# An encoder trunk in one core: the first weight sum of the second layer moves from VectorE to an accumulating transfer

## The chip, the cores and the metric

The kernel runs on one core of one Trainium2 chip. The metric is device time in microseconds (us) for one execution of the whole program, given as the median of several executions. Beside it one execution was recorded by the hardware profiler; its page and trace are what the numbers below come from. The engines are named as the profile names them: PE is TensorE (matmuls), PEld its weight loads, DVE is VectorE, ACT is ScalarE, POOL is GpSimd, SP is SyncE, which here only issues transfers.

## The reference

A two-layer encoder on 512 tokens of width 1024, all in float32. Each layer normalizes the tokens, multiplies them by one wide input matrix, runs a token mixer and an attention into 256 memory tokens, gates the result and adds an output projection:

```python
for i in range(DEPTH):
    h = rmsnorm(x, norm_g[i])
    mem_h = rmsnorm(mem, mem_norm_g[i])
    if i % 2 == 0:
        proj = jnp.einsum('bsd,de->bse', h, w_in_a[j])
        ...
        o_mix = mixer_dilated(qkv, qn_a[j], kn_a[j], ang_a)
    else:
        proj = jnp.einsum('bsd,de->bse', h, w_in_b[j])
        ...
        o_mix = mixer_axial_gqa(proj[..., :c1], proj[..., c1:c2], proj[..., c2:c3],
                                qn_b[j], kn_b[j], ang_b)
    o_mem = memory_attention(q_mem, mem_h, w_mem_kv[i], mem_qn_g[i], mem_kn_g[i])
    y = jnp.concatenate([o_mix, o_mem], axis=-1) * jax.nn.silu(gate)
    x = x + jnp.einsum('bse,ed->bsd', y, w_out[i])
```

The change touches only how the weight matrices of the second layer (`w_in_b` and `w_out[1]`) are prepared for the matmuls.

## The kernel before

**Products.** Float32 accuracy is reached by splitting each operand into a rounded part and a rest: `mm3` (lines 146 to 149) makes three matmuls, rounded by rounded (L147), and the two mixed ones (L148, L149). Most projections are computed in `s_chunk` (line 326) as a two-by-two block product with seven block products in place of eight, in the manner of Strassen and Winograd. That needs sums of the four quarters of a weight matrix. With the quarters called 21, 11, 12 and 22, the sums are T1 = 12 + 11, T2 = 22 + T1, T3 = 12 + 22 and T4 = 21 + T2. The seven products use the operands in the order 21, 11, T1, T2, 22, T3, T4, one after the other; each product of a 512-column chunk is one *group* of 24 matmuls, and PE runs through the groups without a break if nothing is late.

**Chunks.** `PLAN` (line 36) lists the weight chunks in order. The chunks are counted from 0. In the second layer, chunks 20 to 26 (kind W1b) are 512 columns of the input matrix each, in the order memory query, keys and values, two chunks of queries and three of gate; chunk 27 (kind W2b, 1024 columns, two tiles to a quarter) is the first two thirds of the output projection. Chunks 17 and below belong to the first layer; 18, 19, 28 and 29 take no sums.

**Weight pieces.** The class `Weights` keeps a clock `g` that counts groups. `advance` (line 288) is called once per group and puts into the program, in this order: the rest of an earlier piece (`lo`), at most one sum (`sum`), one rounding (`hi`), and the loads (`dma`). A piece of 128x1024 goes through these steps:

- a load from DRAM by SP into a tile `wl` (L217);
- for a sum, the addition into that tile: T1 on DVE (L231); T2 as an accumulating transfer from the T1 tile, issued by POOL (L236); T3 as an accumulating transfer straight from DRAM, issued by POOL (L241); T4 as an accumulating transfer of T2 into the tile of 21 (L246);
- the rounding by ACT into `wh` (L262), two or more groups before the product;
- the rest, `wl - wh`, by DVE into `wo` (L272).

`ripe` (line 219) sets how many groups must lie between a step and the next in the program: `LEAD`, which is 2, after a transfer, and 1 after the DVE sum T1. This is only the order in which instructions are written; at run time each instruction waits by semaphore for what it reads. Every engine works through its own instructions in the written order.

**What else the engines do.** The results of a group leave PSUM through ACT copies (L334) and DVE additions (L344). Head norms take squares on ACT (L495), the inverse root on POOL (L385, L386) and a multiplication on DVE (L500). Rotary terms (L1231 to L1236), softmax (L1280, L1284, L1289, L1290, L1299 to L1308), gates (L698 to L716) and the sums for the output projection (L736 to L762) run between the groups, given out slot by slot by the class `Driver`. POOL's line of work in the second layer is the inverse roots, the rotary table (L1177) and the issuing of T2, T3 and T4, all in one order.

Of the kernel before, what the change touches and what calls it, by code (L numbers as in the profile page):

```python
# [13 lines left out]
ALU = mybir.AluOpType  # L14
# [19 lines left out]
A_ORDER = "01234567mab"  # L34

PLAN = ["W2"] + ["T2"] * 2 + ["W1", "W2s"] + ["W2" if c.isdigit() else "W1" for c in A_ORDER[1:]] + ["W2"] + ["O1"] * 2 + ["T2b"] * 2 + ["W1b"] * 7 + ["W2b"] + ["O1"] * 2
KEEP = {"T2": 6, "T2b": 4, "O1": 4, "W1": 9, "W2": 10, "W2s": 9, "W1b": 7, "W2b": 9}


# [69 lines left out]
def trunk_kernel(ctx: ExitStack, tc: tile.TileContext, x, mem, wall, norm_g, mem_norm_g, gcol,  # L109
                 qn_a, kn_a, qn_b, kn_b, ident_d, mask_d, tab_a, tab_b, out):  # L110
    nc = tc.nc
    V, A, G, T = nc.vector, nc.scalar, nc.gpsimd, nc.tensor
# [26 lines left out]
    def split(hi, lo, src, act=True):  # L139
        if act:  # L140
            A.copy(hi, src)  # L141
        else:
            V.tensor_copy(hi, src)
        V.tensor_tensor(lo, src, hi.bitcast(F32), ALU.subtract)  # L144
# [16 lines left out]
    class Weights:  # L161
        def __init__(self):
            self.items, self.last, self.need, self.allocs, self.sums = [], [], [], [], []
            self.users = {}
            d = g = 0
            for c, kind in enumerate(PLAN):
                base = len(self.items)
                if kind in GROUPS:
                    units, nb = GROUPS[kind]
                    for u in range(units):  # L170
                        for x in (2 * u, 2 * u + 1):
                            self.items.append((c, "P", x))
                            self.last.append(g + (u + 1) * nb - 1)
                            self.allocs.append(((c, "P", x), d, kind))
                            self.users[c, "P", x] = 1
                            d += 1
                        self.need += [base + 2 * u + 2] * nb
                    g += units * nb
                else:
                    n = 1 if kind in ("W1", "W1b") else 2  # L180
                    at = {k: d + i * n for i, k in enumerate(("21", "11", "12", "22"))}
                    d += 4 * n
                    self.allocs += [((c, k, x), at[q] + x, kind) for k, q in LOADS for x in range(n)]
                    for k in ORDER:
                        for x in range(n):
                            self.items.append((c, k, x))
                            self.last.append(g)
                            self.need.append(len(self.items))
                            if k[0] == "T":
                                self.sums.append(((c, k, x), at["22"] + x))  # L190
                            if k != "T4":
                                self.users[c, k, x] = 1 if k in ("22", "T3") else 2
                            g += 1
            assert d == wall.shape[0], (d, wall.shape)
            self.g = -1
            self.live = 0
            self.tile, self.load_at, self.at, self.lo_at = {}, {}, {}, {}
            self.n_hi = self.n_lo = self.taken = 0
            self.op, self.hi_at = [], []
# [8 lines left out]
        def dma(self, most=9):  # L208
            while self.allocs and self.live < KEEP[self.allocs[0][2]] and most:
                most -= 1  # L210
                key, d, _ = self.allocs.pop(0)
                self.live += 1
                self.tile[key] = m4(name="wl")
                self.load_at[key] = self.g
                if key[1][0] != "T":
                    self.at[key] = self.g
                nc.sync.dma_start(self.tile[key], wall[d])  # L217
# [4 lines left out]
        def sum(self, force=False, want=None):  # L222

            for n, (key, d) in enumerate(self.sums[:8]):
                if want and key != want:
                    continue
                c, k, x = key
                if k == "T1":
                    if not (self.ripe(self.load_at, key, force) and self.ripe(self.at, (c, "11", x), force)):
                        continue  # L230
                    V.tensor_tensor(self.tile[key], self.tile[key], self.tile[c, "11", x], ALU.add)  # L231
                    self.use((c, "11", x))
                elif k == "T2":
                    if not (self.ripe(self.load_at, key, force) and self.ripe(self.at, (c, "T1", x), force, 1)):
                        continue
                    G.dma_start(self.tile[key], self.tile[c, "T1", x], accum_op=ALU.add)  # L236
                    self.use((c, "T1", x))
                elif k == "T3":
                    if not self.ripe(self.load_at, key, force):
                        continue  # L240
                    G.dma_start(self.tile[key], wall[d], accum_op=ALU.add)  # L241
                else:
                    if not (self.ripe(self.lo_at, (c, "21", x), force, 1) and self.ripe(self.at, (c, "T2", x), force)):
                        continue
                    self.tile[key] = self.tile[c, "21", x]
                    G.dma_start(self.tile[key], self.tile[c, "T2", x], accum_op=ALU.add)  # L246
                    self.use((c, "T2", x))
                self.at[key] = self.g
                self.sums.pop(n)
                return True  # L250
            return False

        def hi(self, force=False):
            i = self.n_hi
            if i >= len(self.items) or not self.ripe(self.at, self.items[i], force, 1 if self.items[i][1] == "T1" else None):
                return False
            if i >= RING and self.last[i - RING] > self.g:
                return False
            self.n_hi += 1
            wh = pool.tile([128, 1024], F32R, tag="wh", name="wh", bufs=RING)  # L260
            wo = pool.tile([128, 1024], F32R, tag="wo", name="wo", bufs=RING)
            A.copy(wh, self.tile[self.items[i]])  # L262
            self.hi_at.append(self.g)
            self.op.append((wh, wo))
            return True
# [1201 lines left out]
```

## Time and profile before

| what | value |
|---|---|
| median of 3 executions | 1008.05 us (1007.2 to 1014.04) |
| the profiled execution, its own time | 1009.92 us |
| its span, first to last instruction | 1008.1 us |
| PE busy | 961.4 us, 95% of the span |
| DVE busy | 831.5 us, 82% |
| ACT busy | 644.1 us, 64% |
| POOL busy | 331.2 us, 33% |
| T1 on DVE (L231), whole kernel | 33 times, the last at 897.5 us |
| accumulating transfers issued by POOL | 66 from tile to tile, 33 from DRAM, 512 KB each |
| mean rate of all transfers | 200 GB/s |

The second layer's weight chunks 20 to 27 are prepared and used from about 640 us to the end. The profiled execution lasted 1.9 us longer than the median; sums made from its rows are set against its own time first. A busy PE here means that matmuls are in flight; where PE is idle, the profile names the instruction whose end it waited for.

### The profile page before, as it was taken

The numbers are of one execution on the slowest core, as the hardware profiler recorded it, in microseconds if no ns is written. First come the engines' busy times: TensorE is split into PE (matmuls) and PEld (weight loads), VectorE is DVE, ScalarE is ACT, GpSimd is POOL, SyncE is SP. The second block draws the span as 40 slices with busy tenths as digits, with TensorE's granted clock in tenths as the row PEclk, the third lists the DMA queues.
The fourth block names the chain that finished last, engine by engine and source line by source line (L and its number), as shares of the span: only waits on it lengthen the run. The fifth ranks groups of instructions, "written<-read, shape, count | busy, mean of one in ns | idle before, by whom it ended". The sixth has DMA issues, their size and how long they took to land.

```text
span 1008.1 us, 16611 instructions
## 1 busy us (share of the span) xinstructions
PE 961.4 (95%) x5724; PEld 845.4 (84%) x5724; DVE 831.5 (82%) x1496; ACT 644.1 (64%) x1623; POOL 331.2 (33%) x461
## 2 busy tenths in 40 slices
PE   7999999999999999999999889998999889998998
PEld 4779888887878787878899878887999888987886
DVE  6787688778787878787879898979789898889975
ACT  4556578686767676767776665566667566557650
POOL 1223325564545454545552010132631320001000
PEclk9999999999999999999999999999999999999899
DMA  8969936959685858686859593689565745755432
GB/s 337 289 215 353 267 88 174 311 113 263 143 256 143 254 146 252 146 252 155 229 159 312 158 278 134 235 319 271 128 145 144 197 110 173 187 174 139 133 125 84
DMA packets 85670, 201.41 MB, mean 200 GB/s; under 512 B 24913, under 2 KB 35665, under 8 KB 85586
## 3 DMA queue, kind: packets, MB, share of 16 engines
q1 hardware_dynamic: 70034, 146.28, 41.3%
q0 software_dynamic: 14256, 51.91, 27.0%
q10 hardware_dynamic: 1296, 2.16, 0.6%
q8 instruction: 45, 0.74, 0.3%
q14 instruction: 39, 0.32, 0.1%
HBM read 153.07 MB, written 12.65 MB: 164 GB/s over the span
## 4 chain that ended last, share of the span: by engine, by line
PE 55%; DVE 16%; issue 3%; DMA 3%; ACT 2%; POOL 0%; SPq 0%; DVEq 0%; ACTq 0%
PE pj L147 14%; PE pj L148 14%; PE pj L149 14%; DVE wo L272 4%; DVE wl L231 2%; PE oo L1097 1%; PE pt L1076 1%; PE qT L507 1%; DMA oth<-ds 1%; PE sa L995 1%; DVE sn L344 1%; PE ptb L1299 1%; DVE yS L736 1%; PE ob L148 1%; PE ob L149 1%
## 5 line engine op out<-in xcount | busy, mean ns | idle before, releaser
L272 DVE TENSOR_TENSOR wo<-wl,wh 128x1024 fp32r<-128x1024 f32 x255 | 316.6, 1244 | 8.7 <-ACT wh L262 8.6
L262 ACT CAST wh<-wl 128x1024 fp32r<-128x1024 f32 x255 | 267.6, 1056 | 39.9 <-PE pj L149 21.8
L147 PE MATMUL pj<-wh,hS 128*128 128x512 f32 (+1 forms) x448 | 166.4, 371 | 6.2 <-DVE sn L344 6.2
L148 PE MATMUL pj<-wo,hS 128*128 128x512 f32 (+1 forms) x448 | 159.8, 357 | 3.0 <-DVE wo L272 2.9
L149 PE MATMUL pj<-wh,hS 128*128 128x512 f32 (+1 forms) x448 | 159.8, 357 | 0.0
L148 PE MATMUL pj<-wo,h 128*128 128x512 f32 (+1 forms) x336 | 120.2, 358 | 6.3 <-DVE wo L272 6.3
L147 PE MATMUL pj<-wh,h 128*128 128x512 f32 (+1 forms) x336 | 124.0, 369 | 1.6 <-ACT h L141 1.6
L149 PE MATMUL pj<-wh,h 128*128 128x512 f32 (+1 forms) x336 | 119.8, 356 | 0.0
L386 POOL TENSOR_TENSOR rstd<-mse,half 128x4 f32<-128x4 f32 (+2 forms) x98 | 104.5, 1066 | 8.2
L147 PEld LDWEIGHTS pj<-wh,hS 128*128 128x128 f32 x448 | 86.4, 193 | 16.9 <-DVE sn L344 6.9
L148 PEld LDWEIGHTS pj<-wo,hS 128*128 128x128 f32 x448 | 86.6, 193 | 14.3 <-DVE wo L272 4.5
L149 PEld LDWEIGHTS pj<-wh,hS 128*128 128x128 f32 x448 | 86.2, 192 | 12.1
L495 ACT ACTIVATE junk<-sn 128x128 f32<-128x128 f32 x264 | 78.9, 304 | 23.1 <-DVE sn L344 20.6
L385 POOL TENSOR_SCALAR mse<-hss 128x4 f32<-128x4 f32 (+1 forms) x86 | 51.2, 595 | 114.9 <-ACT junk L495 110.4
L334 ACT COPY sn<-pj 128x512 f32<-128x512 f32 x132 | 72.3, 583 | 9.3 <-PE pj L149 9.3
L148 PEld LDWEIGHTS pj<-wo,h 128*128 128x128 f32 x336 | 64.5, 192 | 16.3 <-DVE wo L272 8.9
L246 POOL DMA_DIRECT2D wl<-wl x33 | 29.6, 898 | 142.4 <-DVE wo L272 88.5
L939 POOL TENSOR_TENSOR ta<-sn,tabs 128x128 f32<-128x128 f32 (+1 forms) x64 | 36.5, 571 | 110.2 <-DVE sn L500 77.4
L147 PEld LDWEIGHTS pj<-wh,h 128*128 128x128 f32 x336 | 64.4, 192 | 9.3 <-ACT h L141 2.0
L149 PEld LDWEIGHTS pj<-wh,h 128*128 128x128 f32 x336 | 64.2, 191 | 9.0 <-DVE h L144 0.2
L344 DVE TENSOR_TENSOR sn<-pj,sn 128x512 f32<-128x512 f32 x99 | 67.7, 684 | 3.9 <-PE pj L149 3.9
L147 PE MATMUL pj<-hS,wh 128*128 128x256 f32 x192 | 58.4, 304 | 11.3 <-DVE sn L344 8.7
(225 smaller groups left out, 2457.2 us busy)
## 6 DMA issues: line engine op xcount, KB each, us to landing
wl<-in_wall_dram SPq DMA_DIRECT2D x222, 512.0 KB, 7.1
wl<-wl POOLq DMA_DIRECT2D x66, 512.0 KB, 5.4
wl<-in_wall_dram POOLq DMA_DIRECT2D x33, 512.0 KB, 8.8
od<-o SPq DMA_DIRECT2D x12, 256.0 KB, 4.8
og<-od SPq DMA_DIRECT2D x12, 256.0 KB, 7.0
odb<-o SPq DMA_DIRECT2D x12, 256.0 KB, 2.1
og<-odb SPq DMA_DIRECT2D x12, 256.0 KB, 3.5
x<-in_x_dram SPq DMA_DIRECT2D x4, 512.0 KB, 6.7
```

The costliest lines, as they stand in the source:

```text
L147: T.matmul(o, lh, rh, start=start, stop=False, skip_group_check=True)
L148: T.matmul(o, lh, rl, start=False, stop=False, skip_group_check=True)
L149: T.matmul(o, ll, rh, start=False, stop=stop, skip_group_check=True)
L246: G.dma_start(self.tile[key], self.tile[c, "T2", x], accum_op=ALU.add)
L262: A.copy(wh, self.tile[self.items[i]])
L272: V.tensor_tensor(wo, self.tile[key], wh.bitcast(F32), ALU.subtract)
L334: A.copy(t, b)
L344: V.tensor_tensor(t, b, t, ALU.subtract if q == "12" else ALU.add)
L385: G.tensor_scalar(e, ss, EPS, None, ALU.add)
L386: G.tensor_tensor(r, e, half[:, 0:n], ALU.pow)
L495: A.activation(jk, p[:, j * 128:(j + 1) * 128], AF.Square, scale=QS, accum_out=ss[:, j:j + 1])
L939: G.tensor_tensor(ta[:, 0:n], xn[:, 0:n, 0:32], ropeA[:, 0, b, s0:s0 + n], ALU.mult)
```

## The change

In chunks from number 17 on, T1 is no longer added by DVE. POOL issues a transfer that reads the quarter 11 from DRAM once more and adds it into the tile that holds 12. The tile of 11 that was loaded for its own product is no longer read by the sum. The step from T1 to T2, and from T1 to its rounding, is now written two groups apart as after other transfers, not one. In the first layer (chunks below 17) nothing changes.

```diff
+T1_DMA = 17
 KEEP = {"T2": 6, "T2b": 4, "O1": 4, "W1": 9, "W2": 10, "W2s": 9, "W1b": 7, "W2b": 9}
...
                             if k[0] == "T":
-                                self.sums.append(((c, k, x), at["22"] + x))
+                                self.sums.append(((c, k, x), at["11" if k == "T1" else "22"] + x))
                             if k != "T4":
-                                self.users[c, k, x] = 1 if k in ("22", "T3") else 2
+                                self.users[c, k, x] = 1 if k in ("22", "T3") or k == "11" and c >= T1_DMA else 2
...
                 c, k, x = key
-                if k == "T1":
+                if k == "T1" and c >= T1_DMA:
+                    if not self.ripe(self.load_at, key, force):
+                        continue
+                    G.dma_start(self.tile[key], wall[d], accum_op=ALU.add)
+                elif k == "T1":
                     if not (self.ripe(self.load_at, key, force) and self.ripe(self.at, (c, "11", x), force)):
                         continue
                     V.tensor_tensor(self.tile[key], self.tile[key], self.tile[c, "11", x], ALU.add)
                     self.use((c, "11", x))
                 elif k == "T2":
-                    if not (self.ripe(self.load_at, key, force) and self.ripe(self.at, (c, "T1", x), force, 1)):
+                    if not (self.ripe(self.load_at, key, force) and self.ripe(self.at, (c, "T1", x), force, 1 if c < T1_DMA else None)):
                         continue
                     G.dma_start(self.tile[key], self.tile[c, "T1", x], accum_op=ALU.add)
...
         def hi(self, force=False):
             i = self.n_hi
-            if i >= len(self.items) or not self.ripe(self.at, self.items[i], force, 1 if self.items[i][1] == "T1" else None):
+            if i >= len(self.items) or not self.ripe(self.at, self.items[i], force, 1 if self.items[i][1] == "T1" and self.items[i][0] < T1_DMA else None):
                 return False
```

Line numbers in this document are those of the kernel before unless a text says otherwise; the changed kernel's lines stand one lower from line 37 and five lower from line 229.

## The prediction

> **What bounds the kernel now.** I began with the page: busy times, the granted clock, the chain that ended last.
>
> ```profile
> PE 961.4 (95%) x5724; PEld 845.4 (84%) x5724; DVE 831.5 (82%) x1496; ACT 644.1 (64%) x1623; POOL 331.2 (33%) x461
> ...
> PEclk9999999999999999999999999999999999999899
> ...
> PE 55%; DVE 16%; issue 3%; DMA 3%; ACT 2%; POOL 0%; SPq 0%; DVEq 0%; ACTq 0%
> PE pj L147 14%; PE pj L148 14%; PE pj L149 14%; DVE wo L272 4%; DVE wl L231 2%; PE oo L1097 1%; PE pt L1076 1%; PE qT L507 1%; DMA oth<-ds 1%; PE sa L995 1%; DVE sn L344 1%; PE ptb L1299 1%; DVE yS L736 1%; PE ob L148 1%; PE ob L149 1%
> ```
>
> PE sets the end nearly everywhere. What can be won is PE's idle time, and the few slices where its clock dips; the edited line, L231, is on the chain. Next I cut out the stage of the change (busy time by stage), and asked for L231 in it.
>
> ```profile
> 640.00:932.00 292.00, 272.63 (x1966) 255.84 (x1964) 255.39 (x398) 182.50 (x430) 72.23 (x80) 0.98 0.63 180
> ```
> ```profile
> L231 DVE TENSOR_TENSOR wl<-wl x9: 1219/1219/1223, 676.1 to 897.5; 128x1024 f32<-128x1024 f32 x9
> ...
>   POOL wl L236: 43.1, 2
> ```
>
> The columns of the first row are stretch, length, then busy PE, PEld, DVE, ACT, POOL, clock, DMA share, GB/s. PE idles 292.0 - 272.6 = 19.4 us here, DVE 36.6 us. Nine T1 sums take 9 x 1.22 = 11.0 us of DVE. So the gain is not 11 us by itself: it is what these nine have to do with PE's idle time. The chain in order of time, and PE's idle places (in brackets idle time and what ended it), tell that.
>
> ```profile
> 676.23 1.13 DVE wl L231
> ...
> 702.27 0.93 DVE wl L231
> ...
> 749.04 1.14 DVE wl L231
> ...
> 782.56 1.14 DVE wl L231
> ...
> 813.32 1.14 DVE wl L231
> ...
> 854.20 1.14 DVE wl L231
> ```
> ```profile
> 678.11 0.30 PE L437 MATMUL xT<-ident,xs 128*128 128x128 f32 x1 [0.40 <-DVE xs L472]
> ...
> 704.28 0.38 PE L147 MATMUL pj<-wh,hS 128*128 128x256 f32 x1 [2.30 <-DVE sn L344]
> ...
> 751.43 0.39 PE L147 MATMUL pj<-wh,hS 128*128 128x256 f32 x1 [0.66 <-DVE sn L344]
> ...
> 786.95 0.39 PE L147 MATMUL pj<-wh,hS 128*128 128x256 f32 x1 [3.28 <-DVE sn L344]
> ...
> 817.71 0.39 PE L147 MATMUL pj<-hS,wh 128*128 128x256 f32 x1 [3.19 <-DVE sn L344]
> ...
> 856.60 0.39 PE L147 MATMUL pj<-hS,wh 128*128 128x256 f32 x1 [2.36 <-DVE sn L344]
> ...
> 894.75 0.39 PE L147 MATMUL pj<-hS,wh 128*128 128x256 f32 x1 [0.45 <-DVE sn L344]
> ```
>
> Six of the nine sums (chunks 20, 21, 23 to 26) are on the chain, and each time PE sits idle 1.9 to 4.4 us later for a DVE result queued behind the sum, mostly the L344 that empties a PSUM bank. The sum is written at the start of a product group that needs a fresh bank, so DVE is behind at just that place.
>
> **The change part by part.**
>
> *Removed: nine DVE sums.* Each takes 1.22 us alone and 1.14 us in a row of DVE work. Each place gives the smaller of 1.14 us and PE's idle time: 0.40 (chunk 20), 1.14 (21), 0 (22: no idle place follows), 0.66 (23), 1.14, 1.14, 1.14 (24 to 26), 0.45 (27, first half), 0 (27, second half). Sum 6.07 us. The last zero has this row as its reason: after the ninth sum the chain runs through ACT, which waits for a store of an attention output, not through DVE.
>
> ```profile
> 895.27 4.19 DMA odb<-o
> ```
>
> What is late next in the four large places is still DVE, 1.2 to 2.1 us behind, so each 1.14 us is whole. Bounds: 3 us, if in half of the places another input of the same L344 is nearly as late; 6.07 us above.
>
> *The clock.* Busy time of PE in stretches of 3.41 us, the grid on which the granted clock changes in this trace:
>
> ```profile
> 702.41:705.82 3.41, 1.54 (x13) 1.00 0.29 117
> 705.82:709.23 3.41, 3.41 (x19) 0.50 0.44 154
> 784.33:787.74 3.41, 0.79 (x6) 1.00 0.58 129
> 787.74:791.15 3.41, 3.41 (x18) 0.50 0.96 243
> 815.05:818.46 3.41, 0.75 (x6) 1.00 0.43 84
> 818.46:821.87 3.41, 3.41 (x18) 0.50 1.04 180
> 852.59:856.00 3.41, 1.65 (x12) 1.00 0.92 323
> 856.00:859.41 3.41, 2.81 (x23) 1.00 1.04 302
> ```
> ```profile
> 712.64:716.05 3.41, 3.41 (x31) 1.00 0.96 153
> ```
>
> (The number behind PE's busy time is its matmuls; the next one the clock.) After a stretch with 1.54 us of PE work or less the clock is halved for the next; after 1.65 us it is not. A halved stretch holds 18 or 19 matmuls where a full one holds 31, so it costs 12.5/31 x 3.41 = 1.4 us. Three of the idle places pay this: those of 2.30, 3.28 and 3.19 us. Shortened by 1.14 they are 1.16, 2.14 and 2.05 us. The first can no longer leave under 1.65 us of work in a stretch (3.41 - 1.16 = 2.25), so its halved stretch goes for certain. The other two need more than about 1.8 us of their idle time inside one stretch; on a grid of 3.41 us that happens for about half of all positions ((3.41 - 2.14 + 2 x 0.34)/3.41 = 0.57 for the first). I take one of the two as gone: 2 x 1.4 = 2.8 us. Bounds 0 and 4.2.
>
> [...]
>
> *Added: nine accumulating transfers from DRAM on POOL.* The trace has the very same operation, T3:
>
> ```profile
> L241 POOL DMA_DIRECT2D wl<-in_wall_dram x9: 868/919/1234, 683.4 to 928.8; - x9
> ...
> DMA to landing us min/median/max: 5.3/6.5/11.9
> ```
>
> Issuing costs POOL 9 x 0.92 = 8.3 us; POOL is busy 72 of 292 us and waits for ACT most of the time, so I cost that at nothing. In the built order no new issue stands directly ahead of an inverse root on which DVE waits, but in chunk 22, where it moves one by 0.9 us, and there the T2 issue that stood ahead of the following pair leaves. The orders of PE, ACT and SP are unchanged; DVE's lacks nine rows and nothing else moves.
>
> *The new wait.* T2 (POOL) waits for T1 to land, where it waited for a DVE sum. Behind it on POOL stand T3, T4 and the next inverse roots. In chunks 20 to 25 T2 is written one group later. The tightest is chunk 22, where groups are short:
>
> ```profile
> 724.86 1.86 POOL L386 TENSOR_TENSOR rstd<-mse,half 128x4 f32<-128x4 f32 x1
> ...
> 729.01 0.92 POOL L236 DMA_DIRECT2D wl<-wl  x1
> ...
> 730.32 1.04 POOL L386 TENSOR_TENSOR rstd<-mse,half 128x4 f32<-128x4 f32 x1
> ...
> 784.89 0.93 POOL L236 DMA_DIRECT2D wl<-wl  x1
> ```
> ```profile
> DMA to landing us min/median/max: 8.1/8.1/8.1
> ```
> ```profile
> 740.64 1.06 ACT L262 CAST wh<-wl 128x1024 fp32r<-128x1024 f32 x1
> ...
> 803.91 1.05 ACT L262 CAST wh<-wl 128x1024 fp32r<-128x1024 f32 x1
> ```
>
> (The 8.1 us is the landing of the T2 at 729.01.) The new T1 is issued behind the root at 724.86, at 726.7, and lands 6.5 us later at 733.2. T2 follows at once, after the root of 730.32, 4.2 us later than now; it lands at 741.3, and ACT's rounding of T2 stands at 740.64: 0.7 us late. All of these shift together with PE. From chunk 23 on the groups are longer: in chunk 24 there are 19.0 us between T2 (784.89) and its rounding (803.91), in chunk 22 11.6. I take 1.0 us for chunks 20 and 22 together. Bounds: 0, and with both landings at their longest (11.9 here, 8.1 for T2) 726.7 + 20.0 - 740.64 = 6.1 us.
>
> *Sum.* -6.1 - 2.8 + 1.0 = -7.9 us. The profiled execution took 1009.9 us, so it would become 1002.0. The median stands 1.9 us lower, 1008.05, and becomes **1000.2 us**, -0.8%.
>
> **The rivals.**
>
> 1. *The sum above*: 1000 us.
> [...]
> 3. *Half of the idle time has a second cause*: the PSUM bank is emptied by DVE, but DVE's earlier steps wait in turn for ACT or POOL. Lower bound of both terms: -3.0 - 1.4 + 1.0, 1004.6 us. For it: L500 ahead of two of the L344 needs an inverse root from POOL. Against it: the chain goes from L231 to L344 by DVE alone.
> 4. *All three halved stretches go and the late T2 costs nothing*: -6.1 - 4.2, 997.8 us.
> 5. *Slower: T2 of chunk 22 lands so late that ACT stops.* Between the new issue (726.7) and the rounding (740.64) lie 13.9 us for two landings in a row; 14.6 are forecast. ACT takes its instructions in order, so the copies out of PSUM wait behind the rounding and PE runs out of banks: every further us costs about one. At 22.8 us for the two, the gains of 6.1 + 2.8 = 8.9 us are used up. With nine more transfers beside the loads both landings might double, to 29.2: 15.3 us late, less the 8.9, 1014 us. For it: T3 needed up to 11.9 us. Against it: the DMA share in the stage is 0.63. [...]
>
> That the change doesn't do what it says is excluded by the built order: nine L231 rows are gone.
>
> **How the numbers follow.** Rival 1 0.45, rival 2 0.20, rival 3 0.14, rival 4 0.14, rival 5 0.07. About 1% (10.1 us) is what a measurement of this kernel can tell from no change. Faster by over 1% (under 998.0) is most of rival 4 and the lower edge of rival 1: 0.20. Slower by over 1% (above 1018.1) is the upper part of rival 5 and mechanisms not listed: 0.05. Within 1%: 0.75. The range leaves out the far part of rival 4 and most of rival 5, and reaches above to where rival 5 has used up the gains but for 1 us: 995.5 to 1007.0.
>
> **What would show it.** L231 nine fewer and DVE about 11 us less busy; the idle places before L344 in chunks 21, 24, 25 and 26 shorter by about 1.1 us each; fewer stretches at clock 0.50 between 700 and 860 us; new POOL waits of T2 for a transfer, a few us each. ACT waiting at L262 for a transfer, above all in chunk 22, would be rival 5. Idle places as long as before, with POOL or ACT as the releaser, would be rival 3. I would be wrong most plainly if new idle places appeared on PE near 740 us.

## The result and the profile after

The changed kernel takes 999.97 us (median of 6 executions, 998.17 to 1001.93) where the kernel before takes 1008.06 us (6 executions, 1005.79 to 1014.04): ratio 0.9908, 95% interval 0.9882 to 0.9934. The forecast was 1000.2 us. The profiled execution took 1000.03 us, of which the span is 998.3 us; that of before 1009.92 and 1008.1 us.

The page of the changed kernel, busy times, granted clock and the chain that ended last (L232 is now the new transfer, L236 the DVE sum, L241 T2, L251 T4, L267 the rounding, L349 the DVE addition that empties a PSUM bank):

```profile
PE 955.1 (96%) x5724; PEld 839.7 (84%) x5724; DVE 821.6 (82%) x1487; ACT 644.5 (65%) x1623; POOL 340.2 (34%) x470
...
PEclk9999999999999999999999999999999999999999
...
PE 55%; DVE 14%; DMA 3%; ACT 3%; issue 3%; POOL 1%; SPq 0%; DVEq 0%; ACTq 0%; POOLq 0%
PE pj L149 13%; PE pj L148 13%; PE pj L150 13%; DVE wo L277 4%; PE oo L1102 1%; PE pt L1081 1%; DVE wl L236 1%; PE qT L512 1%; PE sa L1000 1%; DMA oth<-ds 1%; PE ptb L1304 1%; DVE sn L349 1%; DMA wl<-wl 1%; POOL tabs L1182 1%; PE xT L442 1%
```

DVE has nine instructions and 9.9 us less, POOL nine instructions and 9.0 us more. The slice at 8 is gone from the clock's line, and a transfer from tile to tile (`wl<-wl`) and the rotary table on POOL (L1182) are new on the chain. The stage of the change, busy time by stage (columns as in the prediction):

```profile
640.00:922.80 282.80, 268.93 (x1966) 252.87 (x1964) 246.32 (x391) 182.45 (x430) 80.24 (x90) 0.99 0.74 202
```

With the same 1966 matmuls it is 9.2 us shorter: PE idles 13.9 us in place of 19.4, and is busy 3.7 us less, most of which is the clock (PE is busy 3.4 us in a halved stretch, at 784.42 for 18 matmuls, work that takes 2.0 at full clock, where a stretch holds 31). PE's idle places in it:

```profile
702.59 0.39 PE L148 MATMUL pj<-wh,hS 128*128 128x256 f32 x1 [1.17 <-DVE sn L349]
...
727.71 0.39 PE L148 MATMUL pj<-wh,hS 128*128 128x256 f32 x1 [0.95 <-ACT sn L339]
...
782.84 0.39 PE L148 MATMUL pj<-wh,hS 128*128 128x256 f32 x1 [2.15 <-DVE sn L349]
...
812.51 0.39 PE L148 MATMUL pj<-hS,wh 128*128 128x256 f32 x1 [2.06 <-DVE sn L349]
...
848.75 0.39 PE L148 MATMUL pj<-hS,wh 128*128 128x256 f32 x1 [1.23 <-DVE sn L349]
```

The four large places (chunks 21, 24, 25, 26) are shorter by 1.13 us each; those of 0.40, 0.66 and 0.45 us are gone; one of 0.95 us, ended by an ACT copy, is new at 727.71. The clock (busy time of PE in stretches of 3.41 us, its matmuls, the clock):

```profile
702.54:705.95 3.41, 3.37 (x28) 1.00 0.96 354
705.95:709.36 3.41, 3.41 (x31) 1.00 0.38 148
781.01:784.42 3.41, 1.58 (x13) 1.00 0.62 165
784.42:787.83 3.41, 3.41 (x18) 0.50 0.74 287
...
808.29:811.70 3.41, 2.15 (x16) 1.00 0.81 191
811.70:815.11 3.41, 2.60 (x21) 1.00 0.59 117
815.11:818.52 3.41, 3.41 (x29) 1.00 0.69 135
```

Of three halved stretches between 700 and 860 us one is left, at 784.42. The idle place of 2.06 us is now cut in two by the grid (2.15 and 2.60 us of work), and the clock stays.

**A measure free of the first layer.** The same first layer runs up to 1.9 us earlier or later from one profiled execution to the next (chunk 21's idle place, unchanged in e5_other_four, ends there at 702.01 us and in the kernel before at 704.28, of which 0.40 is the place of chunk 20). So I compare traces by the time from the first of the four large idle places (chunk 21) to the last (chunk 26), start to start: before 856.60 - 704.28 = 152.3 us, changed 848.75 - 702.59 = 146.2 us, 6.2 less. The prediction's steps inside this piece give 0.66 + 3 x 1.14 (idle) + 2 x 1.4 (clock) - 1.0 (late T2) = 5.9. The piece is one profiled execution of each kernel; the ratios below are of all executions, each against executions of the kernel before taken beside it (their medians: 1007.3 us for e1 to e4, 1008.3 for e5 to e8, 1008.4 for e9 and e10), so two kernels are better compared by their ratios than by their medians.

| kernel | median us | ratio to before, 95% | piece, us | halved stretches in the piece |
|---|---|---|---|---|
| before | 1008.06 | | 152.3 | 3 |
| changed | 999.97 | 0.9908 (0.9882 to 0.9934) | 146.2 | 1 |
| e1_order_only | 1007.82 | 1.0001 (0.9990 to 1.0012) | 152.3 | 3 |
| e2_no_sum | 998.57 | 0.9916 (0.9900 to 0.9932) | 148.7 | 2 |
| e3_both | 1011.08 | 1.0040 (1.0026 to 1.0054) | 152.6 | 3 |
| e4_four_idle | 1002.09 | 0.9951 (0.9933 to 0.9968) | 146.0 | 0 |
| e5_other_four | 1003.49 | 0.9961 (0.9947 to 0.9976) | 151.3 | 3 |
| e6_table_early | 995.73 | 0.9883 (0.9867 to 0.9898) | 144.9 | 1 |
| e7_all_chunks | 995.73 | 0.9876 (0.9860 to 0.9892) | 146.7 | 1 |
| e8_filled_idle | 1005.73 | 0.9978 (0.9964 to 0.9992) | 147.8 | 0 |
| e9_all_early | 994.86 | 0.9848 (0.9821 to 0.9876) | 145.3 | 1 |
| e10_table_only | 1008.46 | 0.9992 (0.9976 to 1.0007) | 152.4 | 3 |

### The profile page after: what moved, and what is told of

It reads as the page before. It is cut to its first block, busy times and chain, and to the rows that moved or that the text cites. A ratio compares the mean times of both kernels' runs of the same rounds, so it can differ in the third digit from the quotient of the medians.

```text
span 998.3 us, 16623 instructions
## 1 busy us (share of the span) xinstructions
PE 955.1 (96%) x5724; PEld 839.7 (84%) x5724; DVE 821.6 (82%) x1487; ACT 644.5 (65%) x1623; POOL 340.2 (34%) x470
## 4 chain that ended last, share of the span: by engine, by line
PE 55%; DVE 14%; DMA 3%; ACT 3%; issue 3%; POOL 1%; SPq 0%; DVEq 0%; ACTq 0%; POOLq 0%
PE pj L149 13%; PE pj L148 13%; PE pj L150 13%; DVE wo L277 4%; PE oo L1102 1%; PE pt L1081 1%; DVE wl L236 1%; PE qT L512 1%; PE sa L1000 1%; DMA oth<-ds 1%; PE ptb L1304 1%; DVE sn L349 1%; DMA wl<-wl 1%; POOL tabs L1182 1%; PE xT L442 1%
## 5 line engine op out<-in xcount | busy, mean ns | idle before, releaser
L267 ACT CAST wh<-wl 128x1024 fp32r<-128x1024 f32 x255 | 267.6, 1056 | 41.2 <-PE pj L150 20.8
L148 PEld LDWEIGHTS pj<-wh,hS 128*128 128x128 f32 x448 | 85.2, 190 | 14.9 <-DVE sn L349 3.8
L149 PEld LDWEIGHTS pj<-wo,hS 128*128 128x128 f32 x448 | 85.5, 191 | 13.9 <-DVE wo L277 4.1
L150 PEld LDWEIGHTS pj<-wh,hS 128*128 128x128 f32 x448 | 85.3, 190 | 12.1
L390 POOL TENSOR_SCALAR mse<-hss 128x4 f32<-128x4 f32 (+1 forms) x86 | 47.9, 557 | 109.8 <-ACT junk L500 105.3
L251 POOL DMA_DIRECT2D wl<-wl x33 | 29.8, 903 | 131.1 <-DVE wo L277 70.3
L349 DVE TENSOR_TENSOR sn<-pj,sn 128x512 f32<-128x512 f32 x99 | 67.6, 683 | 3.9 <-PE pj L150 3.9
```

Of the source, the lines that this page charges most:

```text
L148: T.matmul(o, lh, rh, start=start, stop=False, skip_group_check=True)
L149: T.matmul(o, lh, rl, start=False, stop=False, skip_group_check=True)
L150: T.matmul(o, ll, rh, start=False, stop=stop, skip_group_check=True)
L349: V.tensor_tensor(t, b, t, ALU.subtract if q == "12" else ALU.add)
L390: G.tensor_scalar(e, ss, EPS, None, ALU.add)
```

## The experiments

My theory was the prediction's: the gain is DVE time taken from ahead of the L344 (now L349) that PE waits for, plus the clock that shorter idle places keep. Rivals: the later place of T2 and the rounding in the written order makes the gain; the clock has no part in it; the transfers themselves cost something.

**The order alone.** The kernel before, with T2 and the rounding of T1 written two groups behind T1, as in the changed kernel:

```diff
-    ... self.ripe(self.at, (c, "T1", x), force, 1)):
+    ... self.ripe(self.at, (c, "T1", x), force, 1 if c < 17 else None)):
...
-    ... force, 1 if self.items[i][1] == "T1" else None):
+    ... force, 1 if self.items[i][1] == "T1" and self.items[i][0] < 17 else None):
```

> The kernel before, with the DVE sum T1 kept, but T2 written one group later in chunks 20 to 26, as the change does; DVE's order is that of before, POOL's differs by the places of the T2 issues. Theory (the gain is DVE time in front of idle PE, and the clock that follows): no gain, 1007 to 1010 us, the idle places of 2.30, 3.28, 3.19 and 2.36 us unchanged. Rival (POOL's inverse roots, no longer behind a T2 issue, are what helps): 1000 to 1003 us.

Measured: 1007.82 us, ratio 1.0001. PE's idle places of this kernel, the first and the last of the four:

```profile
703.46 0.39 PE L147 MATMUL pj<-wh,hS 128*128 128x256 f32 x1 [2.30 <-DVE sn L344]
...
855.80 0.39 PE L147 MATMUL pj<-hS,wh 128*128 128x256 f32 x1 [2.36 <-DVE sn L344]
```

Both are as long as before, and so is the piece between them. The written order alone is not the cause of the gain. It does move T2 and T4, though, and that matters below, where the rotary table is moved.

**No sum at all.** The changed kernel without the new transfer; nothing takes its place:

```diff
-                    G.dma_start(self.tile[key], wall[d], accum_op=ALU.add)
+                    pass
```

> The changed kernel without the nine new transfers: in chunks 20 to 27 the sum T1 is left out, 12 is used in its place, so this part of the computation is missing; everything else stands as in the changed kernel. If the transfers cost what the trace of after shows (one idle place of 0.95 us near 727 us, and that not by the transfer of T1 itself, which had landed 7 us earlier than it was needed): the time of after within 1 us, 999 to 1001. If nine more transfers slow the others: 996 to 998.

Measured: 998.57 us, ratio 0.9916; the time lies between the two ranges that were named. The interval lies inside that of the changed kernel (0.9882 to 0.9934), so the nine transfers have no cost that these runs can tell from nothing. The rounding of T4 in chunk 21 on ACT, and PE's idle place behind it:

```profile
725.71 1.05 ACT L267 CAST wh<-wl 128x1024 fp32r<-128x1024 f32 x1 [2.86 <-DMA wl<-wl]
```
```profile
728.46 0.52 PE L148 MATMUL pj<-wh,hS 128*128 128x256 f32 x1 [1.98 <-ACT sn L339]
```

The new idle place is here too, longer, with no new transfer in the kernel. So it does not come of waiting for the new transfers. What this kernel shares with the changed one is the missing DVE sums and the later written order; the order alone (e1_order_only) has no such place.

**Transfer and DVE time both.** The changed kernel, with DVE adding two halves of 480 columns of the tile of 11 into a tile that nobody reads:

```diff
                     G.dma_start(self.tile[key], wall[d], accum_op=ALU.add)
+                    for s_ in (slice(0, 480), slice(480, 960)):
+                        V.tensor_tensor(scr, self.tile[c, "11", x][:, s_], self.tile[c, "11", x][:, s_], ALU.add)
```

> The changed kernel with a DVE addition of about the old length put back in the old place (two of 128x480 from the tile of 11 into a scratch tile, nine times), so that only the transfers and the later T2 are new against before. Theory: the gain is gone, 1007 to 1010 us, with the idle places near 702, 783, 813 and 849 us back at 2.2 to 3.2 us. Rival (the gain is in POOL's order or in the wait): about 1000 us.

Measured: 1011.08 us, ratio 1.0040, so the whole gain is gone and 3 to 4 us with it. The idle places are back, each 0.12 to 0.14 us longer than before, as two additions (0.66 us each) are longer than one (1.22 us):

```profile
703.79 0.39 PE L148 MATMUL pj<-wh,hS 128*128 128x256 f32 x1 [2.43 <-DVE sn L352]
...
786.86 0.58 PE L148 MATMUL pj<-wh,hS 128*128 128x256 f32 x1 [3.41 <-DVE sn L352]
...
902.05 0.38 PE L148 MATMUL ob<-pbT,vb 128*128 128x256 f32 x1 [1.05 <-ACT pbT L1311]
```

It is DVE's time that makes them. Of the 3 to 4 us above the kernel before, 7 x 0.13 and the new place of 1.05 us at 902.05 explain about 2. Another 1.5 is the size of the clock: its mean over the ten executions is 0.9897, against 0.9915 over the 22 of before beside them, about one halved stretch more in each execution (one is 0.0017 of the time).

**Four chunks with large idle places, and the other four.** The transfer in chunks 21, 24, 25, 26 only, and in 20, 22, 23, 27 only:

```diff
-T1_DMA = 17
+T1_DMA = (21, 24, 25, 26)
...
-                if k == "T1" and c >= T1_DMA:
+                if k == "T1" and c in T1_DMA:
```

> The transfer only in chunks 21, 24, 25 and 26, those whose DVE sum stood ahead of idle places longer than 1.14 us. Theory: 4 x 1.14 = 4.6 us of idle time and the clock's 2.8 us, less up to 1 us for the late transfer: 1000.7 to 1002.5 us. Rival (each DVE sum is worth the same, 8.1/9 = 0.9 us): 1004.5 us.

> The transfer only in chunks 20, 22, 23 and 27, five sums, whose idle places were 0.40, none, 0.66, 0.45 us and none. Theory: -1.5 us and nothing from the clock, 1006 to 1008 us. Rival (each DVE sum is worth 0.9 us): 1003.6 us.

Measured: 1002.09 us (0.9951) and 1003.49 us (0.9961). The two together, 4.9 + 3.9 = 8.8 thousandths, are about the 9.2 of the whole change. By the times alone the rival, 0.9 us for every sum, isn't out: the second is what it said (1003.6) and outside my 1006 to 1008, and the interval of the first, 1001.3 to 1004.8 us by its ratio, holds its 1004.5. What speaks against it are the places in the traces, and e7_all_chunks below, where it said 983 us. PE's idle places with the first four:

```profile
701.94 0.38 PE L148 MATMUL pj<-wh,hS 128*128 128x256 f32 x1 [1.17 <-DVE sn L349]
...
727.58 0.39 PE L148 MATMUL pj<-wh,hS 128*128 128x256 f32 x1 [0.76 <-ACT sn L339]
...
749.23 0.39 PE L148 MATMUL pj<-wh,hS 128*128 128x256 f32 x1 [0.66 <-DVE sn L349]
...
783.62 0.39 PE L148 MATMUL pj<-wh,hS 128*128 128x256 f32 x1 [2.15 <-DVE sn L349]
```

and with the other four:

```profile
702.01 0.39 PE L148 MATMUL pj<-wh,hS 128*128 128x256 f32 x1 [2.30 <-DVE sn L349]
...
783.65 0.39 PE L148 MATMUL pj<-wh,hS 128*128 128x256 f32 x1 [3.28 <-DVE sn L349]
...
853.30 0.58 PE L148 MATMUL pj<-hS,wh 128*128 128x256 f32 x1 [2.36 <-DVE sn L349]
```

Each place shrinks where its own chunk's sum left DVE, and nowhere else: 0.66 us stays in the first and 2.30 us in the second. With the first four no stretch in the piece is halved, though idle places of 2.15 us stand in it; with the other four all three stay. The other four gain more than I expected: the idle places that go are worth 0.40 + 0.66 + 0.45 = 1.5 us, the piece is 1.0 us shorter, and the runs say 3.9 us (2.4 to 5.3). Its profiled execution, 1007.14 us, is 2.8 us below that of before and the slowest of its seven. Two more pieces of the gain are on record. A place of 0.32 us at 901.59 in the trace of before goes too (see the sum below). And the mean clock is 0.9924 against 0.9904 in the 18 executions of before beside it, 1.2 halved stretches fewer, or 1.6 us. With these it is 3.4 us. Why the clock is better when the three large idle places stay, the runs don't show; that my forecast had nothing for the clock here was wrong.

**The idle time filled.** The kernel before, with 14 matmuls of 256 columns, whose results nobody reads, ahead of the L344 waits that stand behind the DVE sums of chunks 21, 24 and 25 (PE is then one chunk earlier); DVE is untouched:

```diff
+                if fill and i == 3:
+                    f = at("fill")
+                    for _ in range(fill):
+                        T.matmul(f[:, 0:256], wh[:, 0, 0:128], wh[:, 0, 0:256], start=True, stop=True)
...
-    s_chunk(256, H2, ev_qmb)
+    s_chunk(256, H2, ev_qmb, fill=14)
```

> The kernel before, with 14 additional matmuls (1.7 us at full clock) into an unused PSUM tile put into PE's order ahead of the three matmuls that waited 2.30, 3.28 and 3.19 us; the sums stay on DVE. PE still waits for the same DVE results. If less than about half a stretch of PE work halves the clock: the three halved stretches go or become rare, 1004 to 1006 us. [...] If the additional matmuls themselves come late: up to 5 us slower, with idle time after them.

Measured: 1005.73 us, ratio 0.9978. PE's idle places, and its busy time on the grid of this trace:

```profile
703.54 0.39 PE L147 MATMUL pj<-wh,hS 128*128 128x256 f32 x1 [0.62 <-DVE sn L344]
...
784.74 0.38 PE L147 MATMUL pj<-wh,hS 128*128 128x256 f32 x1 [1.61 <-DVE sn L344]
...
813.99 0.39 PE L147 MATMUL pj<-hS,wh 128*128 128x256 f32 x1 [1.50 <-DVE sn L344]
...
851.37 0.39 PE L147 MATMUL pj<-hS,wh 128*128 128x256 f32 x1 [2.36 <-DVE sn L344]
```
```profile
811.48:814.89 3.41, 1.91 (x16) 1.00 0.49 96
814.89:818.30 3.41, 3.41 (x28) 1.00 1.02 166
...
848.99:852.40 3.41, 1.05 (x9) 1.00 1.01 375
852.40:855.81 3.41, 3.41 (x18) 0.50 0.87 160
```

The fillers win PE nothing but the clock. All three halved stretches of the piece go, and it is 152.3 - 147.8 = 4.5 us shorter: 1.5 us for each, where I had estimated 1.4. The place of 2.36 us, left unfilled, now lies inside one stretch (1.05 us of work) and pays for it at 852.40, just behind the piece; so the whole gains two stretches, 2.8 us by the estimate and 2.2 (0.8 to 3.6) by the ratio. The mean clock says the same: 0.9942 over twelve executions against 0.9904 over 18 of before, 2.2 stretches fewer. The clock is part of the account.

**The table earlier.** The new idle place at 727.71 stands behind the rounding of T4 in chunk 21, as in e2_no_sum. POOL's instructions before and after the change, in order of time:

```profile
703.71 6.97 POOL L1177 TENSOR_TENSOR tabs<-tbraw,grB 128x512 f32<-128x512 f32 x4 [13.88 <-DMA wl<-in_wall_dram]
710.64 0.87 POOL L236 DMA_DIRECT2D wl<-wl  x1
...
715.78 0.86 POOL L246 DMA_DIRECT2D wl<-wl  x1 [1.89 <-DVE wo L272]
```
```profile
692.32 1.23 POOL L232 DMA_DIRECT2D wl<-in_wall_dram  x1
702.02 7.98 POOL L1182 TENSOR_TENSOR tabs<-tbraw,grB 128x512 f32<-128x512 f32 x4 [8.47 <-DVE grB L1179]
...
711.40 0.94 POOL L241 DMA_DIRECT2D wl<-wl  x1
...
716.59 0.86 POOL L251 DMA_DIRECT2D wl<-wl  x1 [3.34 <-DVE sn L343]
```

and ACT's of after:

```profile
724.96 1.05 ACT L267 CAST wh<-wl 128x1024 fp32r<-128x1024 f32 x1 [1.84 <-DMA wl<-wl]
...
727.10 0.56 ACT L339 COPY sn<-pj 128x512 f32<-128x512 f32 x1
```

In both kernels T2 of chunk 21 (710.64, 711.40) stands on POOL behind the rotary table. In the changed kernel PE is 1.7 us earlier there (702.59 against 704.28), but the table takes 1.0 us longer, a root has come between it and T2, and T2 and T4 are issued 0.8 us later than before. T4 then needs 8.3 us to land (5.8 before). ACT waits 1.84 us for it, the copies behind it come late, and PE idles 0.95 us.

Most of this delay is already in e1_order_only, which has nothing but the later written order. Its T2 and T4 of chunk 21, and the rounding of T4:

```profile
712.11 0.94 POOL L236 DMA_DIRECT2D wl<-wl  x1
...
717.46 0.85 POOL L246 DMA_DIRECT2D wl<-wl  x1 [3.49 <-DVE sn L338]
```
```profile
725.82 1.05 ACT L262 CAST wh<-wl 128x1024 fp32r<-128x1024 f32 x1 [0.35 <-PE pj L149]
```

Counted from the end of PE's idle place of chunk 21, T4 is issued 11.5 us later in the kernel before (715.78 - 704.28), 14.0 in e1_order_only (717.46 - 703.46) and 14.0 in the changed kernel (716.59 - 702.59). Its landing takes 5.8, 8.1 and 8.3 us. So in the kernel before T4 lies ready 5.1 us ahead of its rounding (726.63), and in e1_order_only 0.3 us ahead. The later order has used up nearly all the time in hand, without a cost yet. In the changed kernel the stretch behind 702.59 runs at full clock, PE is 1.4 us earlier against the same idle place, and T4 is late. To see whether the table's place matters, I moved the table three slots forward, ahead of T1 of chunk 21, in the changed kernel and, as a control, in the kernel before:

```diff
-... {"a": 3, "b": 3, "o": 0}, 11
+... {"a": 3, "b": 3, "o": 0}, 8
```

> The changed kernel with the rotary table of the second layer (one DVE scaling, four POOL products of 8 us in all) written three slots earlier, so that T2 of chunk 21 no longer queues behind it on POOL; the new transfer of chunk 21 then stands behind the table. If the idle place of 0.95 us near 727 us came from T2 and T4 of chunk 21 being held by the table: it goes, 998.5 to 999.5 us. If it came from slow landings alone: unchanged, 1000 us, or worse if T1 of chunk 21 now lands late.

> The kernel before, all T1 sums on DVE, with the rotary table of the second layer put on POOL three slots earlier, ahead of the sums of chunk 21. Theory A (the table costs only where T2 must wait for a transfer behind it, so only in the changed kernel): no change, 1008 us, ratio 0.999 to 1.001, and the idle places of 2.3, 3.3, 3.2 and 2.4 us stand as they are. Theory B (the table's 7 to 8 us on POOL slow DVE beside it or push the roots, whoever adds T1): the same gain as it had in the changed kernel, 3 to 4 us, 1004 to 1005 us, with the first idle place (704 us) shorter.

Measured: 995.73 us (0.9883) in the changed kernel, 1008.46 us (0.9992) in the kernel before. POOL in the changed kernel with the early table:

```profile
691.06 6.95 POOL L1182 TENSOR_TENSOR tabs<-tbraw,grB 128x512 f32<-128x512 f32 x4 [0.18 <-DVE grB L1179]
697.95 0.88 POOL L232 DMA_DIRECT2D wl<-in_wall_dram  x1
705.49 0.94 POOL L241 DMA_DIRECT2D wl<-wl  x1 [1.42 <-DMA wl<-in_wall_dram]
```

T2 goes out 5.9 us earlier (4.0 against PE), the idle place at 727 us is gone, and the piece is 1.3 us shorter. In the kernel before the same move does nothing: its idle places are 2.17, 3.28, 3.19 and 2.36 us, as its T4 was in time. So the late T4 of chunk 21 is a wait that the change itself made, by the later written order and by PE running at full clock behind 702.59; with the early table T4 has landed 2.9 us ahead of its rounding (718.6 and 721.53). No kernel here lacks the DVE sums and keeps the old order, so how much of the place each of the two alone would leave is not shown. The early table came out faster than the 998.5 to 999.5 us that I had named: 4 us below the changed kernel by the medians, 2.5 by the ratios, whose intervals overlap. The trace accounts for 1.3 of them.

**From chunk 5 on, and both.** The transfer in the first layer's sums too, and that with the early table:

```diff
-T1_DMA = 17
+T1_DMA = 5
```

> The transfer in the chunks of the first layer too, from number 5 on: 19 more DVE sums gone, 19 more transfers. Theory (a DVE sum is worth only what idle PE stands behind it): the first layer has about 0.75 us of idle PE per chunk that waits for DVE, ended by the rest L277 and not by L349, so 0 to -5 us against the changed kernel if nothing lands late, and worse if T2 waits on the busier POOL queue: 995 to 1003 us. Rival (each sum is worth 0.9 us anywhere): 983 us.

> Both steps that each gave about 4 us over the changed kernel in one: T1 by transfer from chunk 5 on (the first layer's sums too) and the rotary table earlier on POOL. Theory A (they act at different places, 560 us and 728 us): the gains add, 991 to 993 us. Theory B (the late T2 of chunk 21 is already in time, or out of time again, when PE comes 6 us earlier): no more than either alone, 995 to 996 us.

Measured: 995.73 us (0.9876), and 994.86 us (0.9848) for both, the fastest kernel of this study. The first large idle place in the second layer comes at 695.66 us with all chunks from 5 on, against 702.59: 6.9 us earlier, so the first layer gains too, but far less than the rival's 983 us. Its idle place behind the late T4 is longer (1.50 us at 721.33), with the early table it is gone. Whether the two gains add isn't settled: 995.73 and 994.86 say hardly, the ratios (0.9876 and 0.9848, intervals that overlap) say partly, and the piece, 146.7 against 145.3 us, says 1.4 us.

## Why the prediction was right

*The idle places.* Forecast -6.07 us: 0.40, 1.14, 0, 0.66, three times 1.14, 0.45, 0. Measured in the trace: 0.40, 1.13, 0, 0.66, three times 1.13, 0.45, and for the ninth sum, put at nothing, 0.32: PE's idle place at 901.59 in the trace of before is gone in every kernel that takes the sums of chunk 27 off DVE, and stands at 0.29 to 0.34 us in every kernel where DVE still spends that time. Every place behaved by its own chunk (e4_four_idle, e5_other_four), came back with the DVE time (e3_both) and ignored the order (e1_order_only). Rival 3, a second cause for half of the idle time, is out.

*The clock.* Forecast -2.8 us, two of three halved stretches. In the trace two of three went, and the one that the prediction called certain, behind 704.28, was among them. That the clock is worth 1.4 to 1.5 us a stretch, e8_filled_idle shows. It is the least steady term: e4_four_idle, with the same 2.15 us idle place, has no halved stretch in the piece at all, and the mean granted clock of all executions rose from 0.9910 (40 of before, beside the first eight experiments) to 0.9930 (6 of the changed kernel), which is 0.0020 / 0.0017 = 1.2 stretches (one is half of 3.41 us in 1008, 0.0017), or 1.6 us. By that mean the clock term was sized 1.2 us too large. The profiled execution of before, at 0.985, had more halved stretches than most. In the trace of before the stretches at half clock followed those that held the places of 3.28, 3.19 and 2.30 us, each place shorter than one stretch, with 0.79, 0.75 and 1.54 us of PE work left in them. In the twelve traces of the kernels told of here all 23 stretches at half clock between 700 and 860 us followed one with 0.51 us (e3_both, 782.94) to 1.58 us (changed kernel, 781.01) of PE work.

*The late T2.* Forecast +1.0 us for chunks 20 and 22. The size was right (0.95 us), by luck: the place and the cause were not. In chunk 22 the transfers went out as forecast but were quicker than the sum had it: T1 landed in 7.1 us at 730.0, T2 was issued at 730.59, landed in 4.6 us at 735.2, and its rounding stood at 738.57, 3.4 us later. The step that failed is that I looked for the tightest place among T2's new waits, with the table's 7 us on POOL in chunk 21 left out; there it is T4, the last of the chain of sums, that came late. e2_no_sum shows that this needs no new transfer. e1_order_only shows that the later written order alone issues T4 2.5 us later against PE and leaves 0.3 us in hand of 5.1; the rest is PE coming 1.4 us earlier with the clock kept.

*POOL and the nine transfers at nothing.* Forecast 8.3 us of issue, measured 9.0 us more busy time; e2_no_sum, without them, is no faster than the changed kernel by more than the intervals. POOL did not wait for ACT most of the time, as the prediction has it: between 640 and 932 us of the trace of before it waited 82 us for ACT and 110 for DVE, 43 of these for two of the sums that the change removes. Rival 5 did not come about: landing stayed between the bounds.

```profile
L232 POOL DMA_DIRECT2D wl<-in_wall_dram x9: 865/930/1227, 673.1 to 883.5; - x9
...
DMA to landing us min/median/max: 5.4/6.8/11.8
```

*The sum.* Idle 6.1, clock 2.8, new idle place 0.95: 7.9 us of the 9.9 by which the profiled executions differ. Between 857 and 908 us of the trace of before another 0.9 us go that I had not counted, of which the place at 901.59 is 0.32, and 0.7 us behind 932 us, where the trace of before has two halved stretches (931.10 to 937.92) and that of the changed kernel one. The median fell by 8.1 us against a forecast of 7.9. With the clock's mean in place of its trace the terms give 6.7, and 7.0 with the place at 901.59, near the lower edge of the ratio's interval (6.7 to 11.9 us); so the agreement to 0.2 us is partly luck, and about 1 us has no cause shown.

## What to carry to other kernels

Here an operation taken off an engine was worth the sum of PE's idle places that its own queue explained, each capped by the operation's length, not its busy time: nine sums of 1.22 us gave 6 us of idle time and not 11. To it came a clock term, where idle places left PE 1.58 us of work or less in a stretch of 3.41 us; treat that term as a draw, as e4_four_idle lost no stretch with the same place of 2.15 us that cost the changed kernel one. Then ask which chain of sums the new written order moves later, and how much time in hand it had, for PE comes earlier too: here T4 behind a table of 7.98 us in POOL's order took back 0.95 us of the gain, and moving the table cost nothing in the kernel before (0.9992, 0.9976 to 1.0007).

## What the hardware showed that I had not expected

- In these twelve traces little lay between a kept and a halved clock: between 700 and 860 us each of the 23 stretches of 3.41 us with 1.58 us of PE work or less (the largest: changed kernel, 781.01) was followed by a halved one, and none with 1.61 us or more. The smallest that kept the clock is in e4_four_idle (columns: PE's busy time, its matmuls, the clock, DMA share, GB/s):

```profile
779.86:783.27 3.41, 1.61 (x14) 1.00 0.86 149
783.27:786.68 3.41, 3.06 (x25) 1.00 0.65 217
```

- Fourteen matmuls whose results nobody uses, in three idle places, made the kernel before faster (0.9978, 0.9964 to 0.9992).
- One accumulating transfer of 512 KB between the same kinds of tiles took 4.6 us (T2, 711.40) and 8.3 us (T4, 716.59) to land, issued within 6 us of one another. With the later written order alone it is the same (e1_order_only, 4.6 and 8.1 us), in the kernel before 4.4 and 5.8. What was different for the second, the runs don't show.
